# The early half of an output projection as seven block products, with weight sums built in DRAM, in a two-layer encoder on one Trainium2 core

## The chip, the cores and the metric

The kernel runs on 1 core of one Trainium2 chip. The core has five engines with a program of their own each: TensorE (PE; its weight loads are shown apart as PEld), VectorE (DVE), ScalarE (ACT), GpSimd (POOL) and SyncE (SP), and 16 DMA engines that serve transfers issued by SP (queue q1 in the profile) and by POOL (queue q0). The metric is the device time of one execution in microseconds (us). The kernel before took 1635.45 us, the median of 3 runs (1635.05 to 1635.98).

## The reference, cut to what matters

512 tokens of 1024 channels go through two layers, all in float32. Each layer is a trunk of three branches (a gated recurrence A, a spatial gating B, a windowed attention C), a gated sum of their projections, an output projection with residual, and an MLP:

```
for l in range(DEPTH):                      # 2 layers
    xn = rms_norm(x, ln1[l])
    z = xn @ w_in[l]
    y_a, y_b, y_c = ...                     # (512, 512) each, from z
    gates = sigmoid(gz)                     # three gates of 1024 channels
    merged = (gates[0] * (y_a @ w_br[l, 0])
              + gates[1] * (y_b @ w_br[l, 1])
              + gates[2] * (y_c @ w_br[l, 2]))
    x = x + merged @ w_out[l]               # (512, 1024) @ (1024, 1024)
    hn = rms_norm(x, ln2[l])
    x = x + square(relu(hn @ w_up[l])) @ w_down[l]
return rms_norm(x, final_norm)
```

The change is in `merged @ w_out[l]` and in what leads to it.

## The kernel before, in words

**Products in three parts.** A float32 product is made of three matmuls in the fp32r format: each operand is split into a high part (a cast on ScalarE) and a low part (the rest, a subtract on VectorE), and high by high, low by high and high by low are added up in PSUM. Weights come in chunks of 128 x 1024 numbers (512 KB): `wload` (L519 to L525) has SP load one into a buffer `wr` (two buffers), and `wsplit` (L541 to L545) casts it into `wh` (L543, ScalarE) and subtracts into `wl` (L544, VectorE), three buffers each. So a chunk costs one load, one cast and one subtract. Activations are split by `split` (L598, L599), 128 x 512 at a time.

**Token-wise projections.** `proj_tok` (L573 to L593) takes four accumulators of 128 tokens by 512 channels (a bank of PSUM each), and for each chunk of weights (256 input channels by 512 output channels) issues 4 x 2 x 3 = 24 matmuls of 128x512 (L590, L591, L592). Branch outputs yC and yA and the output projection `wo` go through it.

**The stage around the change.** For branch B, `merge_b` (L1326 to L1336) works one block d of 128 channels of the gated projection at a time, channels first, while attention and the recurrence run, and stores it to DRAM (`mgd`, L1336, a POOL transfer). Branches C and A are projected with tokens first: the gated sums `mC` of C (L1494) get A's part added (L1527 and L1528) for the early half of the channels (fl = 0) and then for the late half (fl = 1). `turn_sum(fl)` (L1507 to L1519) turns four blocks of that sum on PE (transposes mT, L1512), loads the matching block of branch B (mB, a POOL transfer, L1515), adds the two (L1517, VectorE) and splits the sum. The output projection (L1538 to L1545) has eight chunks per layer: four with output channels fl = 0, with `turn_sum(1)` between the second and the third, and four with fl = 1: 192 matmuls. Its results are added to the residual `xr` by VectorE with factor 0.5 (L1542), squared and summed for the norm (ScalarE) and turned for the MLP (xT, L670; splits L601 and L602).

The MLP is already done with seven block products in place of eight (`seven`, `down`, `left_first` at L700, `left_second` and `left_sums` at L708 to L740, which make the sums of blocks of the left operand). Their weight sums are made by VectorE in SBUF or by adding transfers of POOL; some results are added to the residual by a scaled copy on ScalarE (`dx`, L825) and an adding POOL transfer (L826).

**What sets the order.** Tiles come from pools whose buffers (tags with a number of buffers) are reused in turn, and whose memory is shared by stages that follow each other: a pool that opens waits for the last readers of the pool that it replaces. The class `Order` is a planner: within marked regions (`plan.span(from, head, fed_at)`) it puts the instructions of each engine in an order of its own, by a list schedule with costs and due times, where PE's written order ranks first; outside it the written order stands. One region runs from the end of branch C's projection through the MLP to the next layer's first stage.

Of the kernel before, what the change touches and what calls it, by code (L numbers as in the profile page):

```python
# [62 lines left out]
class Order:  # L63
# [121 lines left out]
    def plan(self, ops, a, b, rank, head, fed_at):  # L185
# [64 lines left out]
        for key in chain:  # L250
            at = self.opened.get(key[0], 0)
            if at >= a:
                under[key] = [t for o in chain if a <= self.closed.get(o[0], 0) <= at for t in self.slots if self.slots[t][0] == o and t in left]
# [4 lines left out]
        def can(n):  # L258
            t, took = 0.0, {}
            for x in n.first:  # L260
                key, bufs = self.slots[x]
                k = took.get(key, 0)
                if given[key] + k != turn[x] or len(spare[key]) <= k:
                    return None
                t = max(t, sorted(spare[key])[k])
                if key in under and turn[x] < bufs:
                    if any(left[o] for o in under[key]):
# [128 lines left out]
def trunk(tc, xT, xt, ws, vec, fnb, bsb, snk, wst, rope, cmask, amask, ident, out):  # L396
# [4 lines left out]
    def pool(**kw):  # L401
# [18 lines left out]
             "yi": 16, "th": 8,  # L420
# [7 lines left out]
    GROUPS = (("m", "m", "c", "c"), ("a", "a", "s", "s"))  # L428
    WR, WB, NZ, NSM, NQ = 2, 3, 2, 3, 9
# [269 lines left out]

    def left_first(new, u):  # L700

        p1 = T("l2", "sh", F32R).rearrange("p (a b) -> p a b", a=2)
        split(u[:, 0:HT], p1[:, 0], p1[:, 1])
        sb_ = plan.tile(part["wq"], [P, 2, HT], F32, tag="sf", bufs=2, name=nm("sf"))
        nc.vector.tensor_tensor(sb_[:, 0], u[:, 0:HT], u[:, HT:], ALU.subtract)
        return {1: (p1[:, 0], p1[:, 1]), "u": u, "s": sb_}
# [8 lines left out]
    def left_sums(new, h, u, v, sb_=None, held=False):  # L715
        V = nc.vector
        a11, a21, a12, a22 = u[:, 0:HT], u[:, HT:], v[:, 0:HT], v[:, HT:]
        if sb_ is None:
            sb_ = plan.tile(part["wq"], [P, 2, HT], F32, tag="sf", bufs=2, name=nm("sf"))
            V.tensor_tensor(sb_[:, 0], a11, a21, ALU.subtract)  # L720
        sa = plan.tile(part["wq"], [P, 2, HT], F32, tag="sf", bufs=2, name=nm("sf"))
# [94 lines left out]
    def down(qd, raw, hs, xr, r2, nr2, done, between, last, inside):  # L816
# [15 lines left out]
        seven(raw, hs, "d", on, between=between, apart=last and qd == 3, inside=inside)  # L832

# [297 lines left out]
    xsrc = xt  # L1131
    xspill = dram.tile([P, 4, D], F32, name="xspill")
# [3 lines left out]
    for l in range(DEPTH):  # L1136
# [123 lines left out]
        if l:  # L1260
            plan.span(from_, 30000.0, 26000.0)
# [19 lines left out]

        oa = []
# [43 lines left out]
        def merge_b(d):  # L1326
# [9 lines left out]
            nc.gpsimd.dma_start(mgd[:, d], m)  # L1336
# [145 lines left out]
        with later(30000):  # L1482
# [5 lines left out]
            for fl in range(2):  # L1488
# [3 lines left out]
                for t in range(4):  # L1492
                    with hp():
                        nc.vector.scalar_tensor_tensor(mcs[fl][t], th[t], 1.0, pts[t], ALU.add, ALU.mult)  # L1494
            tha = [gates("x", 1, fl) for fl in range(2)]
        from_ = plan.mark()
# [6 lines left out]
        end("br")  # L1503
        begin("Y2")


        def turn_sum(fl):  # L1507

            for d in range(4 * fl, 4 * fl + 4):
# [3 lines left out]
                hi, lo = T("yi", "mgh", F32R), T("yi", "mgl", F32R)  # L1513
                m = T("th", "mB")
                nc.gpsimd.dma_start(m, mgd[:, d])  # L1515
                with hp():
                    nc.vector.tensor_tensor(m, m, pt, ALU.add)  # L1517
                    split(m, hi, lo)
                ms[d] = (hi, lo)  # L1519

        ms = [None] * KT
# [16 lines left out]
        for fl in range(2):  # L1538
            pts = proj_tok(ms, "wo", (l, "wo", fl), fl, None if fl else lambda: turn_sum(1))
            for t in range(4):  # L1540
                with hp():
                    nc.vector.scalar_tensor_tensor(xr[t][fl], pts[t], 0.5, xr[t][fl], ALU.mult, ALU.add)  # L1542
                    n2.add(t, fl)
            with hp():
                n2.turn(fl, range(4), "sa" if fl else "cc")  # L1545
# [7 lines left out]
        end("Y1")  # L1553
# [113 lines left out]
        if last:  # L1667
            plan.span(from_, 30000.0, 26000.0)
# [12 lines left out]
def _chunks(w_in, w_br, w_out, w_up, w_down):  # L1681
# [14 lines left out]
    def make(l, kind, *a):  # L1696
# [24 lines left out]
        if kind == "y":  # L1721
            br, fl, i = a
            w = w_br[l][br]
            return rows(w[crows] if br == 2 else w, i * 2 * P, np.arange(fl * S, (fl + 1) * S))
        if kind == "wo":
            return rows(w_out[l], a[1] * 2 * P, np.arange(a[0] * S, (a[0] + 1) * S))
# [69 lines left out]
```

## Time and profile before

The profiled execution took 1635.45 us, and the span of its instructions is 1633.7 us.

| what | before |
|---|---|
| median, lowest, highest of 3 runs | 1635.45, 1635.05, 1635.98 us |
| profiled execution, its span | 1635.45 us, 1633.7 us |
| PE busy | 1619.4 us, 99%, 9713 records |
| VectorE, ScalarE, GpSimd busy | 1368.8, 1096.7, 190.0 us |
| first and last start of `wo` matmuls | 447.6 and 1306.2 us (layers 0 and 1) |
| HBM read, written | 181.57 MB, 16.78 MB |

How to read it: the page gives the busy time of each engine, the span in 40 slices with PE's granted clock and the share of the DMA engines, and a chain of waits, followed back from the last instruction. In the rows in order of time, the columns are start, length, engine, line, operation, output <- inputs, shapes, and the count; in brackets the idle time before and what ended it. Matmuls are pipelined, so rows of PE overlap: the distance between starts is what one costs. In the rows on DMA, the last number is the median time from issue to landing. A layer's attention and the stores of `merge_b` lie at 256 to 420 us and 1067 to 1230 us.

### The profile page before, as it was taken

The page shows a single profiled execution, that of the slowest core. Times are in us where ns is not written, and L with a number is a line of the kernel's source. Part 1 is how long each engine was busy: PE and PEld are TensorE (multiplying, and loading weights), DVE is VectorE, ACT ScalarE, POOL GpSimd, SP SyncE. Part 2 cuts the span into 40 slices and gives each one's busy share as a digit, 9 for nine tenths or more (in the row PEclk, how much of TensorE's full clock was granted, in tenths as well). Part 3 has the DMA queues.
Part 4 walks back from the last instruction along what each step waited for, and adds up shares of the span by engine and source line. Part 5 has one row for each costly group of instructions (what it writes and reads, how often), then busy time and mean ns, then how long its engine had stood idle before and what let it go on. Part 6 is the DMA issues. An engine that isn't in the chain of part 4 may idle for free.

```text
span 1633.7 us, 26073 instructions
## 1 busy us (share of the span) xinstructions
PE 1619.4 (99%) x9713; PEld 1392.4 (85%) x9713; DVE 1368.8 (84%) x2227; ACT 1096.7 (67%) x1911; POOL 190.0 (12%) x265
## 2 busy tenths in 40 slices
PE   9999999999999999999999999999999999999997
PEld 7788888888888998989888888888888888989896
DVE  8788979677749988888999869896787599888888
ACT  7667567676347777777756555887872487777774
POOL 0011000000300111111110210000003001121210
PEclk9999999999999999999999999999999999999999
DMA  8343222322626575756244332223227265766651
GB/s 324 103 146 122 78 90 73 97 97 86 239 96 206 142 187 145 192 148 156 101 159 128 130 114 85 78 85 104 97 80 244 90 209 150 183 154 169 168 129 52
DMA packets 69999, 222.07 MB, mean 136 GB/s; under 512 B 8976, under 2 KB 9232, under 8 KB 69872
## 3 DMA queue, kind: packets, MB, share of 16 engines
q1 hardware_dynamic: 44352, 154.43, 28.4%
q0 software_dynamic: 25088, 65.42, 16.3%
q8 instruction: 76, 1.25, 0.3%
q10 hardware_dynamic: 432, 0.55, 0.1%
q14 instruction: 51, 0.42, 0.1%
HBM read 181.57 MB, written 16.78 MB: 121 GB/s over the span
## 4 chain that ended last, share of the span: by engine, by line
PE 88%; DVE 6%; DMA 2%; issue 2%; ACT 1%; POOL 1%; SPq 0%; POOLq 0%; DVEq 0%; ACTq 0%
PE us L872 6%; PE us L874 5%; PE us L873 5%; PE dA L776 3%; PE dA L777 3%; PE dA L778 3%; PE wo L590 2%; PE f L550 2%; PE f L549 2%; PE gA L778 2%; DVE wl L544 2%; PE f L548 2%; PE wo L592 2%; PE wo L591 2%; PE at L978 2%
## 5 line engine op out<-in xcount | busy, mean ns | idle before, releaser
L544 DVE TENSOR_TENSOR wl<-wq,wh 128x1024 fp32r<-128x1024 f32 x238 | 290.6, 1222 | 42.6 <-ACT wh L543 42.1
L543 ACT CAST wh<-wq 128x1024 fp32r<-128x1024 f32 x238 | 249.6, 1049 | 98.3 <-PE us L873 15.1
L543 ACT CAST wh<-wr 128x1024 fp32r<-128x1024 f32 x156 | 163.5, 1048 | 141.8 <-PE wo L591 37.5
L544 DVE TENSOR_TENSOR wl<-wr,wh 128x1024 fp32r<-128x1024 f32 x156 | 190.6, 1222 | 60.5 <-ACT wh L543 60.1
L872 PE MATMUL us<-xs,wh 128*128 128x256 f32 x448 | 127.2, 284 | 0.0
L874 PE MATMUL us<-xs,wl 128*128 128x256 f32 x448 | 127.0, 284 | 0.0
L873 PE MATMUL us<-xs,wh 128*128 128x256 f32 x448 | 126.9, 283 | 0.0
L826 POOL DMA_DIRECT2D xr<-dx x84 | 72.1, 858 | 396.7 <-ACT dx L825 384.8
L777 PE MATMUL dA<-wh,sh 128*128 128x512 f32 x256 | 100.1, 391 | 0.0
L778 PE MATMUL dA<-wl,sh 128*128 128x512 f32 x256 | 99.9, 391 | 0.0
L776 PE MATMUL dA<-wh,sh 128*128 128x512 f32 x256 | 99.6, 393 | 0.0
L872 PE MATMUL us<-xh,wh 128*128 128x256 f32 x336 | 95.7, 285 | 0.0
L874 PE MATMUL us<-xh,wl 128*128 128x256 f32 x336 | 95.2, 283 | 0.0
L873 PE MATMUL us<-xl,wh 128*128 128x256 f32 x336 | 95.2, 283 | 0.0
L872 PEld LDWEIGHTS us<-xs,wh 128*128 128x128 f32 x448 | 85.9, 192 | 0.4
L874 PEld LDWEIGHTS us<-xs,wl 128*128 128x128 f32 x448 | 86.0, 192 | 0.0
L873 PEld LDWEIGHTS us<-xs,wh 128*128 128x128 f32 x448 | 85.9, 192 | 0.0
L1006 DVE TENSOR_TENSOR ex<-ex 128x512 f32<-128x512 f32 x112 | 75.0, 688 | 3.8 <-ACT kt L997 3.6
L872 PEld LDWEIGHTS us<-xh,wh 128*128 128x128 f32 x336 | 64.4, 192 | 1.5
L873 PEld LDWEIGHTS us<-xl,wh 128*128 128x128 f32 x336 | 64.4, 192 | 0.8
L874 PEld LDWEIGHTS us<-xh,wl 128*128 128x128 f32 x336 | 64.4, 192 | 0.0
L994 ACT ACTIVATE qt<-ex 128x512 f32<-128x512 f32 x56 | 38.0, 678 | 34.6 <-DVE ex L1006 32.8
(440 smaller groups left out, 4897.8 us busy)
## 6 DMA issues: line engine op xcount, KB each, us to landing
wr<-in_ws_dram SPq DMA_DIRECT2D x142, 512.0 KB, 3.5
wq<-in_ws_dram SPq DMA_DIRECT2D x140, 512.0 KB, 4.6
xr<-dx POOLq DMA_DIRECT2D x84, 256.0 KB, 3.6
thd<-zt POOLq DMA_DIRECT2D x32, 256.0 KB, 2.5
gt<-thd POOLq DMA_DIRECT2D x32, 256.0 KB, 3.7
wq<-in_ws_dram POOLq DMA_DIRECT2D x16, 512.0 KB, 6.2
mgd<-mg POOLq DMA_DIRECT2D x16, 256.0 KB, 2.5
mB<-mgd POOLq DMA_DIRECT2D x16, 256.0 KB, 5.8
```

What stands on the lines that cost most here:

```text
L543: nc.scalar.copy(hi, raw)
L544: nc.vector.tensor_tensor(lo, raw, hi.bitcast(F32), ALU.subtract)
L548: nc.tensor.matmul(pt, whi, xhi, start=first, stop=False)
L776: nc.tensor.matmul(pt, xh[:, t], hi[:, c], start=start and k == 0, stop=False, skip_group_check=True)
L777: nc.tensor.matmul(pt, xl[:, t], hi[:, c], start=False, stop=False, skip_group_check=True)
L778: return nc.tensor.matmul(pt, xh[:, t], lo[:, c], start=False, stop=k == 3, skip_group_check=True)
L826: nc.gpsimd.dma_start(xr[t][fl], z, accum_op=ALU.add)
L872: nc.tensor.matmul(pt, hi[:, c], xh, start=n in (1, 2, 7) and k == 0, stop=False, skip_group_check=True)
L873: nc.tensor.matmul(pt, hi[:, c], xl, start=False, stop=False, skip_group_check=True)
L874: nc.tensor.matmul(pt, lo[:, c], xh, start=False, stop=k == 3, skip_group_check=True)
L994: nc.scalar.activation(qt.rearrange(shp, b=nb, h=2), e_q, AF.Exp)
L1006: nc.vector.tensor_tensor(o_ap, o_ap, ap_of(ex, i_, [[istep, 2]] + z), ALU.add)
```

## The change

In each layer, the early half of the projection's input channels (512 of 1024) is computed as a 2 x 2 by 2 x 2 block product with seven products instead of eight, in the manner of the MLP. The blocks are 256 tokens by 256 channels on the left and 256 by 512 weights (a chunk of 512 KB) on the right. Each product is 2 (token tiles) x 2 x 3 = 12 matmuls of 128x512, and the seven are done in the order 1, 2, 6, 7, then `turn_sum(1)`, then 5, 4, 3. The late half stays plain, 2 x 48 matmuls; it goes on adding in the banks of products 2 and 4 for the first output half. That makes 180 matmuls and 11 chunks per layer.

- **Weights.** The chunks of the projection have five buffers of their own (`wz`), in the pool Y2, and are loaded by SP. Products 1, 2 and 3 take chunks as they are; products 4 to 7 take sums of two to four chunks, built in DRAM (`wsd`) by POOL transfers: a copy and then adding transfers, 11 per layer, issued in pairs behind the stores of `merge_b`.
- **Left operands.** The early blocks mB go through `left_first` and `left_second`, whose temporary tiles `sf` now come from Y2 with four buffers there.
- **Results.** Products 1, 6, 7 and 5 leave by a scaled copy on ScalarE (`wx`, four buffers) and an adding POOL transfer into `xr`; product 3 and the plain half by VectorE as before.
- **Surroundings.** Pool Y1 closes before Y2 opens instead of at the end; `yi` has 20 buffers for 16; the planner's region begins before the gates of branch A are loaded, with other start values (24000 and 20000 ns for 30000 and 26000); its rule on pools that replace others counts tiles whose use began ahead of the region.

```diff
-        res += [(l, "wo", fl, i) for fl in range(2) for i in range(4)]
+        res += [(l, "ws", q) for q in range(4)] + [(l, "wo", fl, i) for fl in range(2) for i in range(2)]
...
+    BYDMA, EARLY, ORDER, WZ = (1, 6, 7, 5), (), (1, 2, 6, 7, 0, 5, 4, 3), 5
...
+    SUMS = {7: (1, 2), 5: (0, 1), 6: (0, 1, 2), 4: (0, 1, 3, 2)}
+    def sums_ahead(l):
+        todo = [(n, r, q[r]) for r in range(4) for n, q in SUMS.items() if r < len(q)]
+        def some(mark, count):
+            with behind(mark):
+                for n, r, q in todo[:count]:
+                    nc.gpsimd.dma_start(wsd[l][:, n - 4], ws[CHUNK[l, "ws", q]], accum_op=ALU.add if r else ALU.bypass)
+            del todo[:count]
+        return some
+    def project_out(l, halves, ms, xr, n2, mid):
+        quad = {1: 0, 2: 3, 3: 2}
+        tag = {1: "c", 6: "c", 5: "c", 3: "c", 2: "m", 7: "a", 4: "a"}
+        def weights(src):
+            raw = plan.tile(part["Y2"], [P, CW], F32, tag="wz", bufs=WZ, name=nm("wz"))
+            nc.sync.dma_start(raw, src)
+            return wsplit(raw)
+        def mms(pt, t, xs, w, first, last):
+            for k2 in range(2):
...
+        def add(t, fl, sign, pt, by_dma=False):
+            if by_dma:
+                z = plan.tile(part["Y2"], [P, S], F32, tag="wx", bufs=4, name=nm("wx"))
+                nc.scalar.activation(z, pt, AF.Copy, scale=0.5 * sign)
+                nc.gpsimd.dma_start(xr[t][fl], z, accum_op=ALU.add)
+            else:
+                nc.vector.scalar_tensor_tensor(xr[t][fl], pt, 0.5 * sign, xr[t][fl], ALU.mult, ALU.add)
+        for n in ORDER:
+            if n == 0:
+                mid()
+                continue
+            if n in (1, 2, 7):
+                banks[tag[n]] = [PT(tag[n], "wo") for _ in range(2)]
+            w = weights(ws[CHUNK[l, "ws", quad[n]]] if n in quad else wsd[l][:, n - 4])
+            for p in range(2):
+                pt = banks[tag[n]][p]
+                mms(pt, slice(p * P, (p + 1) * P), [h[n] for h, u in halves], w, n in (1, 2, 7), n not in (2, 4))
+                if n not in (2, 4):
+                    t, fl, sign = {1: (p, 0, 1), 6: (2 + p, 0, 1), 7: (2 + p, 1, -1), 5: (2 + p, 1, -1), 3: (p, 1, -1)}[n]
+                    add(t, fl, sign, pt, n in BYDMA)
+        for fl in range(2):
+            pts = [PT(b, "wo") for b in "sscc"] if fl else banks["m"] + banks["a"]
+            for i in range(2):
+                w = weights(ws[CHUNK[l, "wo", fl, i]])
+                for t in range(4):
+                    mms(pts[t], slice(t * P, (t + 1) * P), ms[2 * i:2 * i + 2], w, fl == 1 and i == 0, i == 1)
+            for t in range(4):
+                add(t, fl, 1, pts[t])
+                n2.add(t, fl)
+            n2.turn(fl, range(4), "sa" if fl else "ma")
...
-            nc.gpsimd.dma_start(mgd[:, d], m)
+            some(nc.gpsimd.dma_start(mgd[:, d], m), 2)
...
+            from_ = plan.mark()
             tha = [gates("x", 1, fl) for fl in range(2)]
-        from_ = plan.mark()
...
+        end("Y1")
         begin("Y2")
...
-                ms[d] = (hi, lo)
+                    if fl:
+                        ms.append((T("yi", "mgh", F32R), T("yi", "mgl", F32R)))
+                        split(m, *ms[-1])
+                    elif d < 2:
+                        halves.append((left_first(None, m), m))
+                    else:
+                        left_second(lambda: T("yi", "mg", F32R), halves[d - 2][0], m)
...
-        for fl in range(2):
-            pts = proj_tok(ms, "wo", (l, "wo", fl), fl, None if fl else lambda: turn_sum(1))
...
+        project_out(l, halves, ms, xr, n2, lambda: turn_sum(1))
...
-        end("Y1")
...
-            plan.span(from_, 30000.0, 26000.0)
+            plan.span(from_, 24000.0, 20000.0)
```

The region's order moves instructions at two places of which the prediction speaks. The first is SP's order of weight loads in layer 0, from the two chunks of yA's late channels on. Before, all chunks follow in their written order: wr_4454 and wr_4484 are yA's late channels, the rest is the projection.

```order
L524 DMA wr_4454<-in_ws_dram 128x1024
L524 DMA wr_4484<-in_ws_dram 128x1024
L524 DMA wr_4543<-in_ws_dram 128x1024
L524 DMA wr_4573<-in_ws_dram 128x1024
L524 DMA wr_4651<-in_ws_dram 128x1024
```

In the change, wr_4494 and wr_4524 are the chunks of yA's late channels, wr_5097 and wr_5131 the first of the MLP, wz those of the projection:

```order
L527 DMA wr_4494<-in_ws_dram 128x1024
L862 DMA wz_4581<-in_ws_dram 128x1024
L862 DMA wz_4607<-in_ws_dram 128x1024
L862 DMA wz_4625<-wsd_215 128x1024
L862 DMA wz_4651<-wsd_215 128x1024
L862 DMA wz_4723<-wsd_215 128x1024
L527 DMA wr_4524<-in_ws_dram 128x1024
L527 DMA wr_5097<-in_ws_dram 128x1024
```

Five loads of the projection, three of them of sums from DRAM, have moved ahead of yA's last chunk.

The second is VectorE's order at the end of the early gated sums of layer 0. Before, wl_4487 is the subtract of yA's last chunk and wl_4546 that of the first chunk of the projection:

```order
L544 TENSOR_TENSOR wl_4487<-wr_4484,wh_4486 128x1024
L1527 SCALAR_TENSOR_TENSOR gt_4290<-gt_4290,yA_4330 128x512
L1527 SCALAR_TENSOR_TENSOR gt_4292<-gt_4292,yA_4331 128x512
L1528 TENSOR_TENSOR mC_4202<-mC_4202,gt_4290 128x512
L1527 SCALAR_TENSOR_TENSOR gt_4294<-gt_4294,yA_4332 128x512
L1527 SCALAR_TENSOR_TENSOR gt_4296<-gt_4296,yA_4333 128x512
L544 TENSOR_TENSOR wl_4546<-wr_4543,wh_4545 128x1024
L1528 TENSOR_TENSOR mC_4203<-mC_4203,gt_4292 128x512
L1528 TENSOR_TENSOR mC_4204<-mC_4204,gt_4294 128x512
L1528 TENSOR_TENSOR mC_4205<-mC_4205,gt_4296 128x512
L1517 TENSOR_TENSOR mB_4409<-mB_4409,mT_4402 128x512
```

In the change (wl_4527 is the subtract of yA's last chunk, wl_4584 of the first product's):

```order
L1611 TENSOR_TENSOR mC_4218<-mC_4218,gt_4309 128x512
L547 TENSOR_TENSOR wl_4527<-wr_4524,wh_4526 128x1024
L1595 TENSOR_TENSOR mB_4421<-mB_4421,mT_4416 128x512
L1595 TENSOR_TENSOR mB_4434<-mB_4434,mT_4429 128x512
L547 TENSOR_TENSOR wl_4584<-wz_4581,wh_4583 128x1024
L1595 TENSOR_TENSOR mB_4447<-mB_4447,mT_4442 128x512
L1595 TENSOR_TENSOR mB_4471<-mB_4471,mT_4466 128x512
L602 TENSOR_TENSOR sh_4424<-mB_4421,sh_4424 128x256
```

The subtract of yA's last chunk has moved from ahead of the early gated sums to between them and the additions mB. The additions, the weight subtracts of the products and the new 256-wide operations follow each other from there.

More of the change, by code (lines that the diff above doesn't have):

```diff
@@ L252, in plan @@
             if at >= a:
-                under[key] = [t for o in chain if a <= self.closed.get(o[0], 0) <= at for t in self.slots if self.slots[t][0] == o and t in left]
+                shut = {o for o, c in self.closed.items() if a <= c <= at}
+                under[key] = [t for t in self.slots if self.slots[t][0][0] in shut and t in self.users]
+                gone.update({t: before.get(self.users[t][-1], 0.0) for t in under[key] if self.users[t][-1] < a})
         start, line, late, serve = {}, {e: [] for e in ready}, head, 0.0
@@ L266, in can @@
                 if key in under and turn[x] < bufs:
-                    if any(left[o] for o in under[key]):
+                    if any(left.get(o) for o in under[key]):
                         return None
@@ L698, in two, with SF @@
         return tuple(x[:, i * HT:(i + 1) * HT] for x in pr)
+    def SF():
+        return plan.tile(part["wq" if "wq" in part else "Y2"], [P, 2, HT], F32, tag="sf", bufs=2 if "wq" in part else 4, name=nm("sf"))
     def left_first(new, u):
@@ L703, in left_first @@
         split(u[:, 0:HT], p1[:, 0], p1[:, 1])
-        sb_ = plan.tile(part["wq"], [P, 2, HT], F32, tag="sf", bufs=2, name=nm("sf"))
+        sb_ = SF()
         nc.vector.tensor_tensor(sb_[:, 0], u[:, 0:HT], u[:, HT:], ALU.subtract)
@@ L718, in left_sums @@
         if sb_ is None:
[L719 removed]
+            sb_ = SF()
             V.tensor_tensor(sb_[:, 0], a11, a21, ALU.subtract)
[L721 removed]
+        sa = SF()
         V.tensor_tensor(sa[:, 0], a22, a21, ALU.subtract)
@@ new lines, in project_out @@
+    def project_out(l, halves, ms, xr, n2, mid):
+        quad = {1: 0, 2: 3, 3: 2}
+        tag = {1: "c", 6: "c", 5: "c", 3: "c", 2: "m", 7: "a", 4: "a"}
+        banks = {}
+        def weights(src):
[4 more added lines that the diff above has]
+            for k2 in range(2):
+                xh, xl = xs[k2]
+                c = slice(k2 * S, (k2 + 1) * S)
+                nc.tensor.matmul(pt, xh[:, t], w[0][:, c], start=first and k2 == 0, stop=False, skip_group_check=True)
+                nc.tensor.matmul(pt, xl[:, t], w[0][:, c], start=False, stop=False, skip_group_check=True)
+                nc.tensor.matmul(pt, xh[:, t], w[1][:, c], start=False, stop=last and k2 == 1, skip_group_check=True)
+        def add(t, fl, sign, pt, by_dma=False):
[28 more added lines that the diff above has]
+            n2.turn(fl, range(4), "sa" if fl else "ma")
@@ L1131, in trunk @@
     xsrc = xt
+    wsd = [dram.tile([P, 4, CW], F32, name=f"wsd{i}") for i in range(DEPTH)]
     xspill = dram.tile([P, 4, D], F32, name="xspill")
@@ L1279, in trunk @@
         nc.gpsimd.dma_start(sin_t, rope[:, 1])
+        some = sums_ahead(l)
         oa = []
@@ L1512, in turn_sum @@
                     nc.tensor.transpose(pt[:, t * P:(t + 1) * P], mcs[fl][t][:, (d % 4) * P:(d % 4 + 1) * P], id_t)
-                hi, lo = T("yi", "mgh", F32R), T("yi", "mgl", F32R)
                 m = T("th", "mB")
-                nc.gpsimd.dma_start(m, mgd[:, d])
-                with hp():
-                    nc.vector.tensor_tensor(m, m, pt, ALU.add)
-                    split(m, hi, lo)
-                ms[d] = (hi, lo)
-        ms = [None] * KT
+                if fl in EARLY:
+                    nc.scalar.copy(m, pt)
+                    nc.gpsimd.dma_start(m, mgd[:, d], accum_op=ALU.add)
+                else:
+                    nc.gpsimd.dma_start(m, mgd[:, d])
+                with hp():
+                    if fl not in EARLY:
+                        nc.vector.tensor_tensor(m, m, pt, ALU.add)
+                    if fl:
[3 more added lines that the diff above has]
+                        halves.append((left_first(None, m), m))
+                    else:
+                        left_second(lambda: T("yi", "mg", F32R), halves[d - 2][0], m)
+        ms, halves = [], []
         for fl in range(2):
@@ L1667, in trunk @@
         if last:
-            plan.span(from_, 30000.0, 26000.0)
+            plan.span(from_, 24000.0, 20000.0)
         else:
```

13 lines of the change are left out of this document (5 added, 8 removed).

## The prediction, on record before the change was run

> **What bounds the kernel now.** I read the page's busy times and slices first, then the chain of waits, then busy time by stretch around the output projection, and last the engines' rows in order of time there.
>
> ```profile
> span 1633.7 us, 26073 instructions
> PE 1619.4 (99%) x9713; PEld 1392.4 (85%) x9713; DVE 1368.8 (84%) x2227; ACT 1096.7 (67%) x1911; POOL 190.0 (12%) x265
> PEclk9999999999999999999999999999999999999999
> PE 88%; DVE 6%; DMA 2%; issue 2%; ACT 1%; POOL 1%; SPq 0%; POOLq 0%; DVEq 0%; ACTq 0%
> ```
>
> TensorE (PE) is busy for 1619.4 of 1633.7 us, at the full granted clock in every slice, and it is 88% of the chain that ended last. The rest of the span is 14 us; no other engine can give back more than that. So what matters is how many matmuls PE has, and whether the new schedule ever leaves it waiting. The stretches around the projection of layer 0 (columns: length; busy us and instructions of PE, PEld, DVE, ACT, POOL; clock; DMA share; GB/s):
>
> ```profile
> 420.00:440.00 20.00, 20.00 (x93) 16.34 (x93) 13.05 (x18) 4.73 (x5) 7.05 (x13) 1.00 0.87 306
> 440.00:460.00 20.00, 19.97 (x97) 16.47 (x96) 13.89 (x21) 6.64 (x9) 1.64 (x3) 1.00 0.41 141
> 1230.00:1250.00 20.00, 20.00 (x95) 16.34 (x94) 13.16 (x18) 4.55 (x6) 8.38 (x16) 1.00 0.92 320
> ```
>
> PE has no hole there in either layer: a matmul taken out is time gained, and a stall put in is time lost. VectorE (DVE) has about 6 us free of 20, ScalarE (ACT) 13, and the DMA engines are 87 to 92% busy just before the projection. The last is where I look for trouble.
>
> **The 24 matmuls.** The early half of the projection falls from 96 matmuls of 128x512 per layer to seven products of 12, or 84; the late half keeps 96. Over two layers 24 go, all of the same shape as those that stay. PE rows of the trace, with nothing but matmuls of this shape between the first two:
>
> ```profile
> 424.62 0.39 PE L590 MATMUL yA<-wh,yh 128*128 128x512 f32 x1
> ...
> 434.82 0.39 PE L590 MATMUL yA<-wh,yh 128*128 128x512 f32 x1
> ...
> 447.58 0.39 PE L590 MATMUL wo<-wh,mgh 128*128 128x512 f32 x1
> ```
>
> Between 424.62 and 434.82 there are 45 steps, so 10.20 / 45 = 0.2267 us each (the 0.39 us of a row overlap). 24 x 0.2267 = **-5.44 us**, a third of a per cent.
>
> **What is queued ahead of the last yA chunk.** In the order of SP, the load of the second weight chunk of yA, late channels, now stands behind five loads of the new weight tiles. Those five wait for the Y2 pool, which opens when the last gated sum mC (L1494) has been read. On VectorE the subtract of that late chunk now stands directly ahead of the first additions mB (turn_sum), and the third group of transposes on PE needs the bank that the first addition frees. The rows (three mC from 423.55 on, a weight subtract, gated sums and the additions; a weight cast; the mB loads; the third transposes):
>
> ```profile
> 423.55 1.95 DVE L1494 SCALAR_TENSOR_TENSOR mC<-gt,yC 128x512 f32<-128x512 f32 x3
> 425.42 1.22 DVE L544 TENSOR_TENSOR wl<-wr,wh 128x1024 fp32r<-128x1024 f32 x1
> 426.56 0.69 DVE L599 TENSOR_TENSOR yl<-on,yh 128x512 fp32r<-128x512 f32 x1
> ...
> 437.19 1.89 DVE L1528 TENSOR_TENSOR mC<-mC,gt 128x512 f32<-128x512 f32 x3
> 439.71 1.28 DVE L1517 TENSOR_TENSOR mB<-mB,mT 128x512 f32<-128x512 f32 x2 [0.63 <-PE mT L1512]
> ```
> ```profile
> 434.83 1.06 ACT L543 CAST wh<-wr 128x1024 fp32r<-128x1024 f32 x1 [4.39 <-PE yA L591]
> ```
> ```profile
> 426.03 4.44 POOL L1515 DMA_DIRECT2D mB<-mgd  x8 [8.63 <-ACT yh L598]
> ```
> ```profile
> 440.55 0.60 PE L1512 MATMUL mT<-id_t,mC 128*128 128x128 f32 x4
> ```
>
> The third transposes start at 440.55, 0.15 us after the first addition ends (439.71 + 0.69). To keep that, the subtract of 1.22 us must start by 439.71 - 1.22 = 438.49 and the cast of 1.05 us by 437.4: the chunk must have **landed by 437.4**. When does it land? Six loads of 512 KB, one behind the other from 425.5 on. The nearest rows are seven such loads of SP in the MLP, issued from 495.44 on, with the medians of landing of the first and the seventh, each asked for by itself:
>
> ```profile
> 495.44 0.81 SPq L839 DMA_DIRECT2D wq<-in_ws_dram  x2
> 496.29 2.02 SPq L533 DMA_DIRECT2D wq<-in_ws_dram  x4
> 498.42 0.38 SPq L839 DMA_DIRECT2D wr<-in_ws_dram  x1
> ```
> ```profile
> wq<-in_ws_dram SPq DMA_DIRECT2D x1, 512.0 KB, 3.6
> ```
> ```profile
> wr<-in_ws_dram SPq DMA_DIRECT2D x1, 512.0 KB, 8.1
> ```
>
> The first lands at 495.4 + 3.6 = 499.0, the seventh at 498.4 + 8.1 = 506.5: 7.5 / 6 = 1.25 us for each. So the sixth lands 3.6 + 5 x 1.25 = 9.85 us after the first issue, at 435.4. But POOL issues the mB loads (256 KB, half of 1.25, or 0.63 us each) from 426.03 on, one every 0.55 us, and two or three go out ahead of the sixth load (issued near 427.2): 436.7 to 437.3. That is the deadline itself. A stall there is 0 if served so, and about 0.6 us a layer with one more mB load ahead.
>
> Whether the queues are served in that order is the question that decides. A load of SP issued at 431.73 behind eight mB loads, alone and with what moved meanwhile (q0 POOL's, q1 SP's):
>
> ```profile
> q0 software_dynamic: 281, 0.91, 88.8%
> q1 hardware_dynamic: 32, 0.13, 12.2%
> ```
> ```profile
> wr<-in_ws_dram SPq DMA_DIRECT2D x1, 512.0 KB, 6.7
> ```
> ```profile
> wr<-in_ws_dram SPq DMA_DIRECT2D x142, 512.0 KB, 3.5
> ```
>
> The first two rows are of 433.2 to 435.8: with both queues waiting, POOL's earlier loads took 89% and the later one of SP 12%, and it landed after 6.7 us, where the median of all such loads is 3.5. That is near to order of issue. The Trainium skill ("DMA: Bandwidth & Descriptors", section Queues, rings and completion order) says that each DMA engine goes round the queue rows that have work, a packet at a time; by that the two would have shared, and this row disagrees, though one row is thin. What the rule would make of the time is the second rival.
>
> **VectorE between the additions and the transposes of the late half.** New work there: splits, 256-wide sums for the left operands, and the next chunks' subtracts. By the changed order, from the first mB addition to the last of the late mC sums, VectorE has 5 weight subtracts, 18 instructions of 512 columns and 10 of 256. Start to start, a subtract is 426.56 - 425.42 = 1.14 us and a 512-wide one 0.62 (three mC from 423.55 to 425.42). A 256-wide one:
>
> ```profile
> L723 DVE SCALAR_TENSOR_TENSOR sf<-sf,u 128x256 f32<-128x256 f32 x16 | 6.7, 421 | 0.2
> ```
>
> is 0.42 us long, about 0.34 start to start with the same overlap. 5 x 1.14 + 18 x 0.62 + 10 x 0.34 = 20.3 us; from 439.7 it ends at 460.0, or at 459.4 if the subtract ahead is done by 439.1. PE starts the projection at 447.58 and reaches the late transposes after four products, 48 x 0.2267 = 10.9 us later, at 458.5; the last mC sum is wanted after six short transposes and a matmul, near 459.4. So this is a second place with a margin of 0.0 to -0.6 us. A stall at the first place moves PE and VectorE alike, so the two don't add in full. I take **0.5 us a layer for both, +1.0**, with 0 and 2 x 1.3 as bounds: 0.6 at each place, and a little.
>
> Everything behind that has room: each later product of 2.7 us (12 x 0.2267) then pays for one subtract of 1.14 and at most two results of 0.62, and ACT with 13 us free of 20 takes the eight scaled copies.
>
> **The DMA work.** Per layer POOL issues 11 transfers of 512 KB from DRAM to DRAM, 4 copies and 7 adds, behind stores of merge_b. The trace has no such transfer. The nearest rows:
>
> ```profile
> xr<-dx POOLq DMA_DIRECT2D x84, 256.0 KB, 3.6
> wq<-in_ws_dram POOLq DMA_DIRECT2D x16, 512.0 KB, 6.2
> mgd<-mg POOLq DMA_DIRECT2D x16, 256.0 KB, 2.5
> ```
> ```profile
> 256.00:420.00 164.00, 163.87 (x1274) 138.65 (x1273) 130.00 (x293) 114.82 (x266) 16.32 (x27) 1.00 0.29 97
> ```
>
> An adding transfer of 256 KB takes 3.6 where a plain one takes 2.5, one of 512 KB from POOL 6.2 against 3.5. In 256 to 420 us the DMA engines are 29% busy; 11 transfers at 1.25 (a copy) to 2 x 1.25 us (an add that reads both) are some 23 us, which makes 29% into 43%. A weight load behind a pair is then late by up to 5 us, and the stage has loads staged in two raw and three split buffers, which cover most of that. POOL itself gains 11 x 0.55 us of issues in 164 us of which it is busy for 16. Lower bound 0 (it cannot gain); upper bound one uncovered pair in four, 3 pairs x 3 us = 9. I take **+0.3**, nearer to the lower end since the share stays below half. The eight results a layer that are added by DMA (3.6 us to landing) are read by the plain half's add some 20 us later: 0, covered by the products between; without them it would be 3 us once. SP issues three loads more a layer (eleven for eight), at 2.02 / 4 = 0.5 us each by its rows above, beside 1.25 us of transfer: 0.
>
> **Smaller gains.** After a block of short transposes the first matmul takes longer:
>
> ```profile
> 459.53 0.50 PE L590 MATMUL wo<-wh,mgh 128*128 128x512 f32 x1
> 459.87 0.39 PE L591 MATMUL wo<-wh,mgl 128*128 128x512 f32 x1
> ```
>
> 0.34 us to the next where 0.227 is the step, 0.11 lost. The new order of PE has 38 such places where the old one has 42: 4 x 0.11 = **-0.4**, between 0 and that.
>
> **Sum.** -5.4 + 1.0 + 0.3 - 0.4 = -4.5. The profiled execution took 1635.45 us (span 1633.7 and 1.75 around it), which is also the median of the runs, so the forecast is **1630.9 us**. Its own range is 1629.6 (no stall at all: -5.8) to 1632.7 (1.3 us lost a layer and 0.4 to the DRAM sums).
>
> **Rivals.**
>
> *VectorE or the late chunk binds.* The margins above are near zero, and they rest on start-to-start times without one wait for ACT between. If each layer loses 1.5 to 2.7 us instead of 0.5, the gain is used up: -5.8 + 0.3 + 3.0 to 5.4 is -2.5 to -0.1: 1633 to 1635.4. For it: the order has little slack at four places within 15 us. Against: VectorE had 6 us free of 20, and the added work is about 5. From 2.7 us a layer on, the change loses.
>
> *The queues share, and the last yA chunk comes late.* Not the order of issue but a fair share between SP and POOL: SP's six loads need 7.5 us of transfer, POOL's eight mB and four xr loads as much; shared, SP's sixth lands at 425.5 + 15 + 2.3 = 442.8 (3.6 - 1.25 = 2.3 is the fixed part) in place of 435.4 to 437.3, 5.4 us behind its deadline, and PE stands still that long in each layer: -5.8 + 0.3 + 10.8 = +5.3, or **1640.8**. With the xr loads held back to after mB, as before did, 2.9 us late: 1635.8. It is slower than before from 2.7 us a layer on. For it: the stretch in which it would happen is the one with DMA share 0.87 and 0.92. Against: the 89 to 12 row.
>
> *The sums in DRAM are dear.* If the adds cost several times those rows and come between the weight loads of attention, up to the 9 us of the bound above are lost there, in place of 0.3: 1634 to 1639.6. For it: no row shows such a transfer. Against: DMA share 0.29.
>
> That the matmuls don't go can be left out: the order of PE has 24 rows fewer and is otherwise the same outside the projection.
>
> **How the numbers follow.** Forecast 0.57, VectorE or chunk 0.22, shared queues 0.12, dear sums 0.09. This kernel's runs lie 0.06% apart, so 0.2% (3.3 us, below 1632.2 or above 1638.7) can be told. Faster: 0.52 of the forecast's 0.57, and 0.06 in all of the others' low ends: 0.58. Slower: 0.08 of the shared queues, 0.05 of the dear sums, 0.02 of the first rival: 0.15. The same: 0.27. The range leaves out under 1629.4 and above 1638.5, which cuts off about half of the two slow rivals and the best tenth of the forecast.
>
> **What would show it.** 24 fewer matmuls and PE busy near 1614; in a right forecast PE has at most two waits a layer under 1 us, at the third transposes mT (behind VectorE's mB) and at the late ones (behind mC). The late chunk lands 9 to 11 us after the first of the five new loads is issued; if 15, the queues share. PE in the attention stage loses no more than the 0.13 us of 164 that it loses now; if it waits there for split weights, the DRAM sums are the cause. I would be wrong if PE shows waits at places that I called covered: at the second, third or fourth product for weights, or at the norm's transposes for a result added by DMA.

## The result, and the profile after

The change makes the kernel slower. Its median is **1644.95 us** (1641.78 to 1645.49, 6 runs), that of the kernel before in the same runs 1635.25 us; the ratio is 1.0056, 95% interval 1.0043 to 1.0069. Forecast were 1630.9 us, faster. The profiled execution is the shortest of the six, 1641.78 us, so it shows some 3 us less than the median; what follows is of it, unless said otherwise.

The page: span, busy time by engine, chain of waits.

```profile
span 1640.0 us, 26186 instructions
PE 1617.2 (99%) x9689; PEld 1391.4 (85%) x9689; DVE 1385.2 (84%) x2261; ACT 1113.2 (68%) x1941; POOL 222.3 (14%) x303
PE 82%; DVE 6%; issue 5%; DMA 3%; ACT 2%; POOL 1%; SPq 0%; POOLq 0%; DVEq 0%; ACTq 0%
```

The 24 matmuls have gone (9713 to 9689), but PE's busy time fell by 2.2 us instead of 5.4, and 8.5 us more of the span are not busy. Stretches around the projection, layers 0 and 1, with the columns as in the prediction (the granted clock is the number behind the five busy times):

```profile
420.00:440.00 20.00, 18.94 (x88) 15.11 (x86) 10.41 (x15) 2.27 (x3) 7.06 (x13) 1.00 0.82 304
440.00:460.00 20.00, 16.19 (x69) 13.39 (x69) 16.73 (x28) 10.23 (x15) 3.39 (x5) 0.91 0.76 241
1230.00:1250.00 20.00, 20.00 (x93) 16.42 (x91) 11.65 (x19) 3.32 (x4) 9.50 (x18) 1.00 0.82 297
1250.00:1270.00 20.00, 14.97 (x63) 12.01 (x62) 13.10 (x24) 6.42 (x9) 2.68 (x6) 0.83 0.75 268
```

PE now has a hole of about 5 us in each layer, and the clock falls there. PE's waits (us in total, times, longest), and the matmuls around the hole of layer 0:

```profile
PE mT L1586 <- DVE mB L1595: 9.9, 2, 5.0
```
```profile
438.54 0.40 PE L595 MATMUL yA<-wl,yh 128*128 128x512 f32 x1
443.81 0.73 PE L1586 MATMUL mT<-id_t,mC 128*128 128x128 f32 x4 [4.87 <-DVE mB L1595]
```

It is the place that the prediction named, the third transposes. What VectorE and ScalarE did meanwhile, and when SP issued:

```profile
434.97 1.89 DVE L1611 TENSOR_TENSOR mC<-mC,gt 128x512 f32<-128x512 f32 x3
441.93 1.23 DVE L547 TENSOR_TENSOR wl<-wr,wh 128x1024 fp32r<-128x1024 f32 x1 [5.07 <-ACT wh L546]
443.07 1.28 DVE L1595 TENSOR_TENSOR mB<-mB,mT 128x512 f32<-128x512 f32 x2
```
```profile
440.86 1.04 ACT L546 CAST wh<-wr 128x1024 fp32r<-128x1024 f32 x1 [16.23 <-DMA wr<-in_ws_dram]
```
```profile
424.45 0.81 SPq L862 DMA_DIRECT2D wz<-in_ws_dram  x2
425.29 1.65 SPq L862 DMA_DIRECT2D wz<-wsd  x3
427.05 16.46 SPq L527 DMA_DIRECT2D wr<-in_ws_dram  x3
```

PE waits for VectorE's first addition, that stands behind the subtract of yA's last chunk, that waits for ScalarE's cast, and the cast for the load. That load was issued at 427.05 (the first of the three in the last row), behind the five wz loads. Taken by itself, its time from issue to landing is

```profile
wr<-in_ws_dram SPq DMA_DIRECT2D x1, 512.0 KB, 13.7
```

so it landed at 440.75, 16.3 us after the first of the five was issued. The prediction had reckoned 9.9 in SP's queue alone and 11.2 to 11.8 with POOL's loads, and had said of 15 that the queues share. From 428 to 441 us, SP's queue (q1) and POOL's (q0), with packets, MB and share of the time of the DMA engines:

```profile
q1 hardware_dynamic: 732, 2.67, 53.2%
q0 software_dynamic: 678, 2.25, 48.2%
```

They share, half and half. A chain of waits drawn for 424 to 446 us alone ends in

```profile
433.87 9.18 DMA mB<-mgd
443.05 0.02 issue
443.07 0.69 DVE mB L1595
```

and so names an mB load. That load is the seventh of POOL's eight, while the first addition adds to the first of them. VectorE's rows above show that the addition followed the subtract ahead of it without a pause, and in experiment 7, with the same order of loads, it runs before the chunk has landed. It was the chunk that was late.

A balance by PE's rows, from the first matmul of yA (late part) to the first of the projection, and from there to the first of the MLP, in us:

| | before | change | chunk first (below) |
|---|---|---|---|
| yA to projection, layer 0 | 422.35 to 447.58: 25.23 | 421.26 to 453.18: 31.92 | 25.23 |
| yA to projection, layer 1 | 1235.07 to 1258.72: 23.65 | 1237.25 to 1268.55: 31.30 | 23.63 |
| projection to MLP, layer 0 | 447.58 to 496.94: 49.36 | 453.18 to 499.31: 46.13 | 46.10 |
| projection to MLP, layer 1 | 1258.72 to 1308.07: 49.35 | 1268.55 to 1314.73: 46.18 | 46.12 |
| MLP of layer 0 to yA of layer 1 | 738.13 | 737.94 | 738.32 |

The projection gains 3.2 us in each layer. Just ahead of it 6.7 and 7.65 us are lost, of which the idle time is 4.9 and 5.0; the rest, 1.8 and 2.6, fits the slower clock behind the hole (last section).

### The profile page after: what moved, and what is told of

Its sections match the earlier page's. It is cut to its first block, busy times and chain, and to the rows that moved or that the text cites. A ratio compares the mean times of both kernels' runs of the same rounds, so it can differ in the third digit from the quotient of the medians.

```text
span 1640.0 us, 26186 instructions
## 1 busy us (share of the span) xinstructions
PE 1617.2 (99%) x9689; PEld 1391.4 (85%) x9689; DVE 1385.2 (84%) x2261; ACT 1113.2 (68%) x1941; POOL 222.3 (14%) x303
## 3 DMA queue, kind: packets, MB, share of 16 engines
q8 instruction: 76, 1.25, 0.3%
## 4 chain that ended last, share of the span: by engine, by line
PE 82%; DVE 6%; issue 5%; DMA 3%; ACT 2%; POOL 1%; SPq 0%; POOLq 0%; DVEq 0%; ACTq 0%
PE us L943 5%; PE us L944 5%; PE us L945 5%; PE dA L782 3%; PE dA L783 3%; PE dA L784 3%; DVE wl L547 2%; DMA mB<-mgd 2%; PE f L553 2%; PE f L552 2%; PE f L551 2%; PE gA L784 2%; PE gA L782 2%; PE gA L783 2%; PE at L1049 2%
## 5 line engine op out<-in xcount | busy, mean ns | idle before, releaser
L546 ACT CAST wh<-wr 128x1024 fp32r<-128x1024 f32 x140 | 146.6, 1047 | 121.2 <-DMA wr<-in_ws_dram 42.1
L547 DVE TENSOR_TENSOR wl<-wr,wh 128x1024 fp32r<-128x1024 f32 x140 | 171.1, 1222 | 47.6 <-ACT wh L546 47.2
```

Of the source, the lines that this page charges most:

```text
L546: nc.scalar.copy(hi, raw)
L547: nc.vector.tensor_tensor(lo, raw, hi.bitcast(F32), ALU.subtract)
```

## The experiments

The theory now: the load of yA's last chunk is late because it stands behind five loads *and* shares the DMA engines with POOL's loads (**place and sharing**). Rivals: with the chunk on time, VectorE's chain is the next to bind; or there are too many bytes to move there, whatever the order; and, ahead of all, that the DRAM sums cost something.

**1. The chunk ahead of the five loads.** In the planner's test of buffers:

```diff
+                if key[1] == "wz" and any(self.users[o][0] < n.at and self.users[o][0] not in start for y in chain if y[1] == "wr" for o in chain[y]):
+                    return None
```

> The change with one rule more in the planner: the loads of the projection's chunks (wz) may start only once the loads of the chunks written ahead of them have, so that yA's last chunk is issued ahead of the five wz loads instead of behind them, in both layers. Theory 'place and sharing' (the stall at the third transposes is yA's last chunk, late because it stands behind five loads that share the DMA engines with POOL's mB and xr loads): the two waits of 4.9 us and the low clock after them go, the 3.2 us a layer that the projection gained stay, 1627 to 1631. Theory 'VectorE is next' (with the chunk on time, the chain to the late transposes has no slack): the gain is used up, 1632 to 1636. Theory 'too many bytes there' (some load is late whatever the order): 1639 or more.

Measured: 1630.27 us, ratio to the kernel before 0.9968 (95% interval 0.9956 to 0.9979). SP's order differs at that load; the planner then also puts its subtract back ahead of the gated sums. The stretches of layer 0:

```profile
420.00:440.00 20.00, 20.00 (x96) 16.32 (x95) 14.12 (x20) 5.25 (x7) 7.05 (x13) 1.00 0.89 325
440.00:460.00 20.00, 20.00 (x99) 16.68 (x97) 19.96 (x34) 13.45 (x20) 5.99 (x8) 1.00 0.98 317
```

No hole is left, and the wait falls out of the list. The DMA engines are as busy as in the change or more, so it is not the bytes, and VectorE is busy for 19.96 of 20 us without holding PE up: the last of its late gated sums ends just ahead of PE's late transposes,

```profile
455.61 1.89 DVE L1613 TENSOR_TENSOR mC<-mC,gt 128x512 f32<-128x512 f32 x3
```
```profile
458.04 1.03 PE L1588 MATMUL mT<-id_t,mC 128*128 128x128 f32 x8
```

at 457.50 against 458.04. Half a microsecond is all the slack there is in layer 0.

**2, 3. Three and four loads ahead instead of five.** `WZ` is the number of wz buffers.

```diff
-    BYDMA, EARLY, ORDER, WZ = (1, 6, 7, 5), (), (1, 2, 6, 7, 0, 5, 4, 3), 5
+    BYDMA, EARLY, ORDER, WZ = (1, 6, 7, 5), (), (1, 2, 6, 7, 0, 5, 4, 3), 3
```

> The change with three buffers for wz instead of five: yA's last chunk stands behind three loads instead of five. Theory 'place and sharing': two loads of 512 KB less ahead, and what POOL moves beside them, 2 x 1.25 x 2 = 5 us earlier, no wait or less than 1 us there: 1629 to 1634 (later products may then wait for their chunk). If the queues were served in order of issue, 2.5 us earlier: 2.4 us of wait left a layer, 1636 to 1640. Theory 'too many bytes there': as the change, 1641 to 1646.

> The change with four buffers for wz: yA's last chunk stands behind four loads, between the three (no wait) and the five (4.9 us) already run. With equal shares for both queues each load ahead costs 2 x 1.25 = 2.5 us: the chunk came 0.9 us before it was needed behind three loads, so behind four the wait is 1.7 us a layer, and the time 1630.4 + 2 x 1.7 = 1634, if PE's clock stays up after so short a wait, up to 1636 if it falls as after the 4.9 us. In order of issue (1.25 a load) the wait would be 0.4 us: 1631.

Measured: three 1630.46 us, ratio 0.9971 (0.9959 to 0.9982), no wait there; four 1635.77 us, 1.000 (0.999 to 1.001). The latency of the chunk behind three and behind four, and the wait behind four:

```profile
wr<-in_ws_dram SPq DMA_DIRECT2D x1, 512.0 KB, 9.7
```
```profile
wr<-in_ws_dram SPq DMA_DIRECT2D x1, 512.0 KB, 12.4
```
```profile
PE mT L1586 <- DVE mB L1595: 5.9, 2, 3.1
```

Each load ahead makes the chunk 2.0 to 3.2 us later, not 1.25: counted from the first wz load, it landed after 11.1 us behind three (425.40 to 436.46), 14.3 behind four (424.63 to 438.93), 16.3 behind five. The wait behind four was 2.9 and 3.1 us where 1.7 was expected, and the clock fell behind it (last section). This profile is the longest of ten executions, 1637.33 us.

**4. The xr loads by SP.**

```diff
-                nc.gpsimd.dma_start(xr[t][fl], xsrc[:, t, fl * S:(fl + 1) * S])
+                nc.sync.dma_start(xr[t][fl], xsrc[:, t, fl * S:(fl + 1) * S])
```

> The change with the residual's loads xr (16 of 256 KB) issued by SP, where they stand behind yA's last chunk, instead of by POOL; the five wz loads stay ahead of the chunk. Theory 'place and sharing': the two or three xr loads that were served before the chunk landed are gone from beside it, 2 to 3 x 0.63 = 1.3 to 1.9 us less wait a layer, 1638 to 1642. If POOL's loads did not matter and place in SP's queue alone did: 1642 to 1646, no change to the wait of 4.9 us.

Measured: 1645.65 us, ratio 1.0061 (1.0047 to 1.0075), outside the range of 'place and sharing' and in that of 'place alone'. The run does not decide for the latter, since POOL's loads did not go from beside the chunk: in layer 0, its next mB loads came up in the place of xr's, so that its queue was never empty. From 428 to 441 us the shares were

```profile
q1 hardware_dynamic: 771, 2.71, 56.4%
q0 software_dynamic: 605, 2.02, 44.1%
```

much as in the change. Taking three loads out of a queue did not help while others waited in it.

**5, 6. One queue, and one queue with VectorE's order held.** The loads of mB too by SP; POOL then loads nothing at that time.

```diff
-                    nc.gpsimd.dma_start(m, mgd[:, d])
+                    nc.sync.dma_start(m, mgd[:, d])
```

> The change with the loads of mB and of xr issued by SP instead of POOL. In SP's order yA's last chunk now stands behind nine loads (the five wz and four mB) instead of five, but no other queue loads at that time. Equal shares between the queues as the cause: the chunk lands 3.5 + 5 x 1.25 + 4 x 0.63 = 12.3 us after the first of the nine instead of 16.3, no wait or under 0.5 us, 1629 to 1632. If the number of loads ahead in SP's own queue were the cause, the wait stays or grows: 1641 or more.

Measured: 1631.34 us, ratio 0.9977 (0.9967 to 0.9986), no wait at the third transposes. The expected landing was missed, 14.2 us after the first load instead of 12.3; yet behind nine loads the chunk's latency from its own issue was

```profile
wr<-in_ws_dram SPq DMA_DIRECT2D x1, 512.0 KB, 9.5
```

9.5 us against 13.7 behind five in the change. But the planner had also put the subtract of the chunk behind VectorE's first two additions, so two things differed. Hence the second run, where the planner has to start that subtract before the two additions, as in the change:

```diff
+        if subs and adds:
+            kept_ = {x: subs[-1:] for x in adds[:2]}
...
+                    if any(o not in start for o in kept_.get(c, ())):
+                        continue
```

> The mB and xr loads issued by SP (as in the run with one queue), and VectorE held to the change's order, with the subtract of yA's last chunk ahead of the first two additions; the run with one queue had let the planner move it behind them, so that two things differed there. With one queue the chunk landed 2.1 us earlier, counted from the start of yA, than in the change; if that is all that the second queue costs, 1.5 to 2.8 us of wait a layer stay at the third transposes: 1633.5 to 1638. If the second queue were the whole cause, no wait: 1630 to 1632.

Measured: 1632.95 us, ratio 0.9986 (0.9976 to 0.9995), between the two ranges. The wait is back, but short:

```profile
PE mT L1595 <- DVE mB L1604: 2.3, 2, 1.3
```

1.1 and 1.3 us in place of 4.9 and 5.0. In layer 0, from the start of yA, the chunk landed after 17.1 us (421.53 to 438.61) instead of 19.5 (421.26 to 440.75): 2.4 us of the wait go with the second queue. Another 1.4 us go since PE's order has the third transposes six matmuls later there, and 1.1 stay. By this balance about half of the 4.9 us is the sharing. The other half, 2.5 us, would stay with PE's order unchanged: it is the place, here behind the nine loads of SP's queue.

**7. VectorE's additions ahead of the subtract**, all loads as in the change: the same edit the other way round, `kept_[subs[-1]] = adds[:2]`.

> The change with SP's and POOL's order untouched (yA's last chunk still behind five loads) and one rule for VectorE: the subtract of that chunk may start only after the first two additions mB, so that the additions no longer wait for the chunk. If the 4.9 us come from the place of the subtract on VectorE as much as from the late load, only PE's own need of the chunk is left: it lands about 440.8, is cast by 441.8 and subtracted by 443.1, and PE wants it near 441.3 and 442, 1 to 1.6 us a layer, too short for the clock to fall: 1632 to 1634. If the late load alone decides, wherever VectorE does the subtract, the wait stays above 3 us: 1638 or more.

Measured: 1636.72 us, ratio 1.001 (1.000 to 1.002). The chunk is as late as in the change, 19.7 us after the start of yA (423.35 to 443.01), and the additions come ahead of it:

```profile
439.57 1.29 DVE L1604 TENSOR_TENSOR mB<-mB,mT 128x512 f32<-128x512 f32 x2 [0.62 <-PE mT L1595]
```

PE's new waits in layer 0 are its own need of the chunk, for the cast and then for the subtract:

```profile
444.22 0.50 PE L602 MATMUL yA<-wh,yh 128*128 128x512 f32 x1 [0.91 <-ACT wh L555]
445.48 0.50 PE L604 MATMUL yA<-wl,yh 128*128 128x512 f32 x1 [0.53 <-DVE wl L556]
```

1.4 us, and 1.6 in layer 1, as expected: VectorE's place for the subtract turned a chunk that was 1.4 us late into a stop of 4.9. The time is nevertheless 2.7 us above the expected range. In the profile (1638.12 us, 1.4 above the median), from yA to the projection 2.0 us are lost in layer 0 and 3.7 in layer 1, where the clock fell; and from the projection to the MLP layer 0 needs 47.5 us instead of 46.1; why was not followed up.

**8, 9. The sums in DRAM.** First the kernel before with the 22 transfers and nothing that reads them:

```diff
-            nc.gpsimd.dma_start(mgd[:, d], m)
+            some(nc.gpsimd.dma_start(mgd[:, d], m), 2)
```

> The kernel before, with only the 22 DRAM to DRAM transfers of the weight sums added (4 copies and 7 adds a layer behind the stores of merge_b); nothing reads their result. Theory 'the sums cost nothing': 1635.0 to 1635.6. Theory 'the sums are dear': 1636.5 to 1640.

Measured: 1635.38 us against 1635.40, ratio 1.0002 (0.9992 to 1.0011). Attention stages of this run:

```profile
256.00:420.00 164.00, 163.87 (x1274) 138.51 (x1274) 129.42 (x290) 114.06 (x266) 24.11 (x37) 1.00 0.48 134
1067.00:1230.00 163.00, 160.87 (x1251) 135.29 (x1250) 130.33 (x290) 122.52 (x270) 22.34 (x34) 1.00 0.47 129
```

Layer 0 is untouched to the hundredth; in layer 1 PE was busy for 1.3 us less than before's 162.13, of which 0.9 are this wait:

```profile
PE sc L1413 <- DVE mx L1416: 0.9, 1, 0.9
```

Ten of the twelve profiles with the sums have it, with 0.3 to 0.9 us; the two of the change have not, nor have the two without sums (before and the next run). Then the other way round, the kernel of experiment 1 with plain chunks in place of the sums, so that its result is not the projection:

```diff
-            w = weights(ws[CHUNK[l, "ws", quad[n]]] if n in quad else wsd[l][:, n - 4])
+            w = weights(ws[CHUNK[l, "ws", quad.get(n, n - 4)]])
```

> The kernel with yA's last chunk first, without the 22 DRAM to DRAM transfers: products 4 to 7 load a plain chunk of the weights in place of the sum, so this leaves the adding of the weight sums out and its result is not the projection. All loads, matmuls and orders outside the sums stay. If the sums are free, the same as with them, 1629.5 to 1631; if the waits of up to 1.3 us that some profiles with sums show in the attention stage of layer 1 come from them, 1628.5 to 1629.5.

Measured: 1628.18 us, ratio 0.9960 (0.9947 to 0.9972), with the sums 0.9968 (0.9956 to 0.9979). That is just under both expected ranges, but the intervals overlap, and the sums alone cost at most 1.8 us by the interval of the run before: a cost between 0 and some 2 us stays open, and is not what made the change slow.

**10, 11. Results added by VectorE**, on top of experiment 1:

```diff
-    BYDMA, EARLY, ORDER, WZ = (1, 6, 7, 5), (), (1, 2, 6, 7, 0, 5, 4, 3), 5
+    BYDMA, EARLY, ORDER, WZ = (), (), (1, 2, 6, 7, 0, 5, 4, 3), 5
```

> The kernel with yA's last chunk first (the planner's rule on wz loads), and with all results of the products added by VectorE instead of ScalarE and POOL: 8 additions of 512 columns a layer more on VectorE, 8 x 0.62 = 5 us, of which some 3 us fall before the late transposes. If VectorE has slack there, 1630 to 1631 as with the adds by DMA; if its margin is the 0 to 0.6 us that the prediction reckoned, PE waits 1 to 3 us a layer: 1632 to 1636.

> Once more, with more rounds: yA's last chunk first and all results added by VectorE, the fastest so far (1629.35). If adding by DMA is worth nothing here, it stays at 1629 to 1631 and is no different from the 1630.3 with the adds by DMA; a clear gain of one over the other would be more than 1 us.

Measured: 1629.35 us, ratio 0.9966 (0.9953 to 0.9979), and 1629.62 us, 0.9969 (0.9958 to 0.9980). No different from adding by DMA, though VectorE has no pause left,

```profile
440.00:460.00 20.00, 20.00 (x95) 16.35 (x94) 20.00 (x35) 10.41 (x14) 1.64 (x3) 1.00 0.77 289
```

and the planner then spreads PE's late transposes from 459.07 to 465.40 us, where experiment 1 has them from 458.04 to 460.88. This and experiment 1 beat the kernel before by about 0.3%, and the change by about 0.9%.

**12. The change once more**, for a second profile.

> The change once more, for a second profile: the profiled execution of 1641.8 us was the shortest of six, the median 1645.0. If the difference lies in the same place, the waits at the third transposes are the same (4.9 to 5.7 us) and the low clock after them lasts longer; if it lies elsewhere, other rows of PE show it.

Measured: 1643.8 us. The waits are 4.5 and 5.5 us, and from yA to the projection 32.30 and 31.12 us pass (31.92 and 31.30 in the first profile): the same two places. The rest of the 2 us lies elsewhere, 1.3 us of it between the MLP of layer 0 and yA of layer 1. No profile shows an execution of 1645 us. Their mean granted clock is 0.994, as in this profile, against 0.996 in the first, so they probably spent more time at the low clock; how much longer that made them is open.

## Why the prediction was wrong, by its own steps

**The bound and the 24 matmuls: right.** PE bounds the kernel, and without the hole the projection stage gains 3.2 us a layer, where 2.72 for the matmuls and 0.2 for the switches were reckoned. With the chunk on time the kernel takes 1630.27 us, and 1630.9 had been forecast. That they lie so near is in part luck: the forecast had 1.0 us of waits in it that did not come, and of the 6.4 us gained at the two projections the medians show 5.1; where the rest went was not traced.

**What is queued ahead of the last yA chunk: the place right, the step after it wrong.** That the chunk stands behind five loads, that VectorE's subtract of it holds up the additions and these the third transposes, and that it had to land by 437.4, all came so; in the change, yA began 1.09 us earlier, so that the limit was 436.3 and the landing at 440.75 was 4.4 us late, for 4.9 of wait. The step that failed is "That is near to order of issue", and with it the landing after 9.85 us, or 11.2 to 11.8 with two or three mB loads ahead. From one load of SP that came behind a full queue of POOL's, and got 12% of the DMA engines to begin with, I took that loads are served as issued. In the change both queues had work waiting from 428 us on, and each got about half (53% and 48%). Each load ahead then cost 2.0 to 3.2 us instead of 1.25, and the chunk landed after 16.3 us. The row was also read over too short a time. Before's row for 432 to 435 us has only POOL's queue at work, and in that for 435 to 436 us SP's load has its half:

```profile
q0 software_dynamic: 364, 1.18, 102.4%
```
```profile
q0 software_dynamic: 70, 0.21, 52.7%
q1 hardware_dynamic: 50, 0.20, 49.7%
```

Why a lone load waits some 3 us behind another queue's work, when two full queues share evenly, no run here settles. The rule of the Trainium skill ("DMA: Bandwidth & Descriptors", section Queues, rings and completion order) that each DMA engine goes round its queue rows was set aside on that thin row; the 53 to 48% agree with it.

**The second rival was the case.** It had the mechanism, 442.8 for the landing (441.8 in before's time) and 5.4 us of standstill (4.9). Its 1640.8 us were 4 too low against the median, and it got a chance of 0.12: the stretch with DMA share 0.87 to 0.92 would have deserved more than one row of evidence against. What it lacked is the clock, which costs 1.8 to 2.6 us a layer more in the profile.

**Both places taken together as +1.0: wrong in size, for the first place alone.** In the profile 14.3 us are lost there over the two layers, the slow clock included. At the second, the late transposes, a margin near zero was about right: experiment 1 shows half a microsecond of slack and no wait. The first rival, with 1.5 to 2.7 us a layer lost to thin margins, did not come: the chunk bound, but by the sharing and for 4.9 us.

**The DMA work (+0.3): within what the runs can tell.** The DMA share of the attention stage of layer 0 rose from 0.29 to 0.49, beyond the 0.43 reckoned. In the change a transfer of the sums lands after

```profile
wsd<-in_ws_dram POOLq DMA_DIRECT2D x22, 512.0 KB, 8.0
```

8.0 us, somewhat more than the 6.2 of the nearest row, and PE lost nothing there in its own profile. The results added by DMA cost nothing that the runs can tell, as reckoned.

**The range** did not hold the time: it ended at 1638.5, below even the 1640.8 at which the rival that came true was priced.

## What to carry to other kernels

When a planner moves loads ahead of one that is needed sooner, work out its landing with every queue that has work at that time taking an equal share, not only with what was issued ahead of it. An engine that takes its instructions in order can multiply the delay: a chunk 1.4 us late for PE became a stop of 4.9 us because its subtract stood ahead of an addition that freed a bank. On a kernel that is 99% TensorE, count behind each hole the time in which the clock is low as well.

## What the hardware showed that I had not expected

**The clock falls behind a hole.** Stretches behind the hole in layer 0 of the change (4.9 us of idle time), behind that with four loads ahead (2.9 us), and around the end of the hole in layer 1 of the change, where PE starts again at 1258.36; the granted clock stands behind the five busy times:

```profile
443.80:445.00 1.20, 1.19 (x7) 1.01 (x8) 1.20 (x2) 0.80 (x2) 0.00 (x0) 0.69 0.85 280
445.00:447.00 2.00, 2.00 (x8) 1.71 (x7) 2.00 (x5) 0.00 (x0) 0.00 (x0) 0.50 0.69 252
447.00:449.00 2.00, 2.00 (x9) 1.62 (x8) 0.66 (x3) 1.39 (x2) 0.55 (x1) 0.83 0.70 217
```
```profile
443.00:445.00 2.00, 2.00 (x9) 1.62 (x8) 1.93 (x4) 0.00 (x0) 0.00 (x0) 0.50 0.89 313
445.00:447.00 2.00, 2.00 (x9) 1.65 (x8) 0.68 (x3) 1.07 (x2) 0.55 (x1) 0.86 0.78 231
```
```profile
1256.00:1258.00 2.00, 0.00 (x0) 0.00 (x0) 1.52 (x2) 1.40 (x2) 0.00 (x0) 0.66 1.01 412
1258.00:1260.00 2.00, 1.64 (x7) 1.46 (x8) 2.00 (x4) 0.81 (x2) 0.00 (x0) 0.50 0.66 199
1260.00:1262.00 2.00, 2.00 (x8) 1.71 (x7) 1.84 (x5) 0.00 (x0) 0.00 (x0) 0.50 0.74 227
1262.00:1264.00 2.00, 2.00 (x8) 1.55 (x7) 0.53 (x2) 1.45 (x2) 0.54 (x1) 0.64 0.47 158
```

Taking a mean between 0.50 and 1.00 as a stretch partly at half, it stands at half for some 3.4 us in the first case (1.20 x 0.62 + 2.00 + 2.00 x 0.34) and for some 6.8 in the third, where it falls within the hole. A matmul then takes 0.43 us from start to start instead of 0.227, and behind these holes 1.6 to 2.6 us are lost beside the idle time. The Trainium skill ("TensorE: Matmul & The Clock Gate", Part 1) puts the fall at a window of about 3.4 us without work; here 2.9 us were enough. Probably they are not always: of the ten executions with four loads ahead, the five of 1636.37 us and more, the profiled one among them, have a mean granted clock of 0.996, and the five of 1635.16 us and less have 0.998, as kernels without the hole; no profile shows the waits of these five. And in layer 1 of experiment 7 waits of 1.0 and 0.5 us, with 0.7 us of work between, were followed by the same:

```profile
1259.00:1262.00 3.00, 3.00 (x9) 2.35 (x8) 3.00 (x5) 1.25 (x2) 0.00 (x0) 0.50 0.79 261
```

while 1.1 and 1.3 us in the two layers of experiment 6, and 1.4 us in layer 0 of experiment 7, were not. What decides for such short waits is open.

**Two full queues share the DMA engines about evenly**, by time (53% and 48%) and nearly by bytes (2.67 and 2.25 MB in 13 us).
